# Head mixers cut into steps with preparation traced one step ahead, and TensorE held to the traced order inside them

## The chip, the cores and the metric

One core of a Trainium2 chip runs the kernel. The metric is the device time of one execution in microseconds (us); less is better. Five engines work side by side, each through its own queue of instructions: TensorE (PE, with its weight loads shown apart as PEld), VectorE (DVE), ScalarE (ACT), GpSimd (POOL) and SyncE (SP), which issues the DMAs.

## What is computed

Two layers of a sequence model over 1280 tokens (256 of context, 1024 latent) of width 1024. A layer is a mixing part and an MLP. What the change touches is the mixing part:

```python
p = modulate(x, shift, scale) @ w_in            # one projection, 20 slices
mixed = (hgrn2_mixer(p), mlstm_mixer(p), retention_mixer(p), gla_mixer(p))
# each: 4 heads, a forward and a backward chunkwise scan, summed:
#   attn = (q k^T, weighted by the decay between t and s), within a chunk
#   o    = attn @ v + (q * exp(b)) @ S          # S: state that enters the chunk
#   S    = exp(b_last) * S + (k * exp(b_last - b))^T v
x = x + g1 * (head_norm(mixed) * gates(p)) @ w_o
x = x + g2 * relu(modulate(x) @ w1)**2 @ w2
```

HGRN2 and GLA have a decay per channel, so their `attn` is built from blocks of halving size (64, 32, 16, 8, 4, 2, then pairs and the diagonal), each with its own scaled copies of q and k. Retention and mLSTM have a decay per head.

## The kernel before

All is in float32. The projections run as three matmuls a product (`mm3`, lines L294 to L296; the weights are split into a high and a low part by `whalf`: one ACT copy L282, one DVE subtraction L283). They go through `denseT` (128 output channels by 256 or 512 tokens, 24 matmuls a block, result into one of three PSUM banks, then an `evac` by ACT and DVE) and `denseV` (L632 to L634).

The mixers and the projections are interleaved by hand. A mixer is a generator that yields a cost in ns. `Fill.along` adds the cost to a debt and takes steps of queued projections (the filler) until the debt is paid; a step is what a projection does up to its own `yield`. `Fill.until` runs filler alone up to a mark. `Fill.also` is a second generator, drawn on in three of five filler steps: `ada_rows`, 128 products on DVE (L414, each with a read of its accumulator) whose 256 KB operands come by DMA, in layer 0 only, from the first HGRN2 pass on.

The passes of a layer, in the order traced, with what the filler holds: GLA (projections of HGRN2's first pair of heads and its values), HGRN2 pair 0 (`spill_hg(1)`: two decay projections and a query, then two gates), HGRN2 pair 1 (the two gates, mLSTM's keys and queries, its values, a gate), then filler alone up to mLSTM's values, two mLSTM passes, two retention passes, and the rest of the filler alone.

In `mix_vec` (GLA and HGRN2) a pass first makes the states (keys: DVE, ACT exp, transposes L893, `state_update` L818, evacuation `evac_states` L1197, a recurrence over chunks `chain` L799 and L803). Then come groups of four chunks (three for GLA). A group makes, for h = 64, 32, 16, 8, 4, 2, the scaled copies F and E (DVE L976 to L991, ACT exp L985 and L989), the products (L1000 for h = 64, L1019 below) and their place in `CTs` (DVE L1032); then `direct(1)` and `direct(0)` (L932 to L956); then the outputs: `out_chunks` multiplies the states (L831, K = 128 rows for a pair of heads, the state kept as a 128-column block whose other head's half is zero) and the values (L834, two tiles of 64 columns), and `finish` norms the result (square, matmul with `bones` L706, ACT, DVE L709) and stores it.

A scheduler of the language takes the traced instructions and fixes each engine's order ahead of the run: it plays the program through by its own costs and gives an engine the earliest traced instruction that is ready by then. So the order on TensorE is not the traced one: filler that was traced later can stand ahead of a mixer's product.

Buffers of the mixers come from `Heap`, a free list with a moving start over two long tiles (px, ph); filler weights lie in `pw`.

Of the kernel before, what the change touches and what calls it, by code (L numbers as in the profile page):

```python
# [8 lines left out]
I32 = mybir.dt.int32  # L9
# [6 lines left out]
NK = 8  # L16
# [140 lines left out]
class Fill:  # L157
# [10 lines left out]
    def step(self):  # L168
        while self.q:
# [28 lines left out]
class K:  # L198
# [36 lines left out]
    def setup(self):  # L235
# [33 lines left out]
        self.late = None  # L269
# [278 lines left out]
    SIZES = {"raw": NC * 48, "V": NC * 256, "V65": NC * 260, "S": NC * 256, "S65": NC * 130}  # L548
# [15 lines left out]
    def denseT(self, tile, tbs, evac):  # L564
# [133 lines left out]
    def finish(self, kt, ps, c0, m):  # L698
# [6 lines left out]
        p2 = self.bank(self.mb.next())[:, 0:n]  # L705
        nc.tensor.matmul(p2, lhsT=self.bones, rhs=sq, start=True, stop=True)  # L706
        nc.scalar.activation(sq, p2, AF.Ln, bias=self.eps)
        nc.scalar.activation(sq, sq, AF.Exp, scale=-0.5)
        nc.vector.scalar_tensor_tensor(y, y, self.ghead[:, self.l, kt:kt + 1], sq, op0=ALU.mult, op1=ALU.mult)  # L709
        nc.sync.dma_start(self.d_y[kt, :, 128 * c0:128 * c0 + n], y)  # L710
# [111 lines left out]
    def out_chunks(self, chunks, pair, qd, ST, at, V, kt):  # L822
# [16 lines left out]
    def mix_vec(self, S, kind):  # L839
# [29 lines left out]
        ST = self.get(S, "S")(NC, 2, 128)  # L869
        gone = [S[x] for x in (("Q", "B0", "B1") + (("G0", "G1") if hg else ("K",)))]  # L870
        gone2 = [S[x] for x in (("S",) if hg else ("S", "V"))]

        for g0, g1 in ((0, 4), (4, 8), (8, 10)):
# [3 lines left out]
            kno = [hp.alloc(n) for _ in range(2)]  # L877
            for d in range(2):
# [9 lines left out]
                if not hg:  # L888
                    nc.vector.tensor_tensor(kf, kf, Kx[:, sl], op=ALU.mult)
                bk = self.mb.next()  # L890
# [3 lines left out]
                nc.scalar.activation(self.v(kno[d], n), self.bank(bk)[:, 0:n], AF.Copy)  # L894
            bk = self.mb.next()
            for d in range(2):
                kn = self.v(kno[d], g1 - g0, 128)
                for i, c in enumerate(range(g0, g1)):
                    f = self.feeds(c, d)
                    if f is None:  # L900
                        continue
                    ps = self.state_update(c, d, kn[:, i, :], V, heads, ST, bk, d * 4 + i, 64)
            self.evac_states(bk, ST, g0, g1, 64, 4, hs)
            hp.free(*kk, *kno)
            yield (g1 - g0) * (220 + 220 * nh)
        self.chain(ST, lambda c, d: dc[d][:, c:c + 1])
# [3 lines left out]
        for g0 in range(first, NC, step):  # L910
# [4 lines left out]
            qo = [hp.alloc(n) for _ in range(2)]  # L915
            qv = [self.v(x, n) for x in qo]
            for d in range(2):
                nc.scalar.activation(qv[d], B[d][:, sl], AF.Exp, scale=esc)
                nc.vector.tensor_tensor(qv[d], qv[d], Q[:, sl], op=ALU.mult)
            ato = hp.alloc(nh * n)  # L920
            AT = self.v(ato, nh * m, 128)
            cto = hp.alloc(nh * m * 32)
            CTs = self.v(cto, nh * m, 32)

            def direct(h):
                do = hp.alloc(n)
                D = self.v(do, n)
                if h == 0 and hg:
                    ao = hp.alloc(n)
                    a = self.v(ao, n)  # L930
                    for d, o in ((0, D), (1, a)):
                        nc.vector.tensor_tensor(o, G[d][:, sl], B[d][:, sl], op=ALU.add)  # L932
                        nc.scalar.activation(o, o, AF.Exp)
# [5 lines left out]
                else:  # L939
# [12 lines left out]
                    nc.vector.tensor_tensor(D2, D2, two(Q[:, sl])[:, :, ::-1], op=ALU.mult)  # L952
# [789 lines left out]
```

## Time and profile before

| | us |
|---|---|
| median of 3 runs (lowest, highest) | 3277.83 (3273.87, 3279.31) |
| the profiled execution: its time | 3277.57 |
| its span, first to last instruction | 3275.8 |
| mixers of layer 0, about 88 to 799 us | 711 |
| mixers of layer 1, about 1873 to 2470 us | 597 |
| PE busy in the whole span | 3188.0 (97%) |
| PEld / DVE / ACT busy | 2607.3 / 2098.3 / 1285.0 |

The stages between and after the mixers (output projection, MLP) are not touched. Matmul ends are modelled, and matmuls overlap one another, so that a busy PE is not a PE at its peak. The two mixer stages are 1308 us of the span, and all that the change can move lies in them. The granted clock is 0.99 of full speed over the span.

### The profile page before, as it was taken

The numbers are of one execution on the slowest core, as the hardware profiler recorded it, in microseconds if no ns is written. First come the engines' busy times: TensorE is split into PE (matmuls) and PEld (weight loads), VectorE is DVE, ScalarE is ACT, GpSimd is POOL, SyncE is SP. The second block draws the span as 40 slices with busy tenths as digits, with TensorE's granted clock in tenths as the row PEclk, the third lists the DMA queues.
The fourth block names the chain that finished last, engine by engine and source line by source line (L and its number), as shares of the span: only waits on it lengthen the run. The fifth ranks groups of instructions, "written<-read, shape, count | busy, mean of one in ns | idle before, by whom it ended". The sixth has DMA issues, their size and how long they took to land.

```text
span 3275.8 us, 52563 instructions
## 1 busy us (share of the span) xinstructions
PE 3188.0 (97%) x20681; PEld 2607.3 (80%) x20681; DVE 2098.3 (64%) x4333; ACT 1285.0 (39%) x2665; POOL 11.5 (0%) x42
## 2 busy tenths in 40 slices
PE   7999999999999999999999999999999999999998
PEld 4787788878888888888888677788778888888887
DVE  4778887776588845454545586876756555555546
ACT  4666564545332121212122575764444322222222
POOL 0000000000000000000000000000000000000000
PEclk9999899999999999999999999999999999999999
DMA  6115566345157511111111212333224111111111
GB/s 208 58 61 176 183 186 190 120 134 179 63 165 230 161 39 39 39 39 39 39 39 40 78 64 73 120 109 113 90 72 151 58 46 52 46 52 46 52 49 65
DMA packets 181953, 308.20 MB, mean 94 GB/s; under 512 B 21880, under 2 KB 51240, under 8 KB 181448
## 3 DMA queue, kind: packets, MB, share of 16 engines
q1 hardware_dynamic: 180376, 303.02, 28.8%
q8 instruction: 162, 2.65, 0.3%
q10 hardware_dynamic: 1296, 1.81, 0.2%
q14 instruction: 87, 0.71, 0.1%
q0 software_dynamic: 32, 0.01, 0.0%
HBM read 259.11 MB, written 45.65 MB: 93 GB/s over the span
## 4 chain that ended last, share of the span: by engine, by line
PE 81%; DVE 8%; DMA 6%; ACT 3%; issue 1%; SPq 0%; DVEq 0%; ACTq 0%
PE psum L294 22%; PE psum L295 21%; PE psum L296 21%; PE psum L831 2%; PE psum L601 2%; PE psum L834 1%; PE psum L818 1%; PE psum L632 1%; DMA ph<-w_adaR 1%; PE psum L634 1%; PE psum L633 1%; PE psum L1359 1%; PE psum L706 1%; PE psum L1019 1%; DMA ps<-w_ada 1%
## 5 line engine op out<-in xcount | busy, mean ns | idle before, releaser
L526 DVE SCALAR_TENSOR_TENSOR x<-psum,st,x 128x512 f32<-128x512 f32 (+1 forms) x648 | 440.7, 689 | 203.5 <-PE psum L296 202.8
L282 ACT ACTIVATE pc<-st 128x512 fp32r<-128x512 f32 x256 | 161.2, 632 | 854.4 <-PE psum L295 840.9
L295 PE MATMUL psum<-pc,pc 128*128 128x512 f32 (+1 forms) x1296 | 477.0, 368 | 6.0 <-DVE pc L506 6.0
L294 PE MATMUL psum<-pc,pc 128*128 128x512 f32 (+1 forms) x1296 | 476.1, 367 | 0.0
L296 PE MATMUL psum<-pc,pc 128*128 128x512 f32 (+1 forms) x1296 | 474.7, 366 | 0.0
L294 PE MATMUL psum<-Hhi,pc 128*128 128x512 f32 (+1 forms) x1280 | 471.1, 368 | 1.5 <-ACT pc L282 1.5
L295 PE MATMUL psum<-Hlo,pc 128*128 128x512 f32 (+1 forms) x1280 | 472.0, 369 | 0.1
L296 PE MATMUL psum<-Hhi,pc 128*128 128x512 f32 (+1 forms) x1280 | 470.5, 368 | 0.0
L294 PE MATMUL psum<-Hhi,pw 128*128 128x512 f32 (+1 forms) x1192 | 451.5, 379 | 7.6 <-ACT pw L282 3.5
L295 PE MATMUL psum<-Hlo,pw 128*128 128x512 f32 (+1 forms) x1192 | 447.5, 375 | 0.0
L296 PE MATMUL psum<-Hhi,pw 128*128 128x512 f32 (+1 forms) x1192 | 446.6, 375 | 0.6 <-DVE pw L283 0.6
L505 DVE TENSOR_TENSOR st<-st 128x256 f32<-128x256 f32 (+1 forms) x160 | 101.8, 637 | 301.5 <-ACT pc L504 300.8
L295 PEld LDWEIGHTS psum<-pc,pc 128*128 128x128 f32 x1296 | 245.0, 189 | 48.4 <-DVE pc L506 6.9
L294 PEld LDWEIGHTS psum<-pc,pc 128*128 128x128 f32 x1296 | 245.0, 189 | 44.1 <-DVE x L526 1.2
L296 PEld LDWEIGHTS psum<-pc,pc 128*128 128x128 f32 x1296 | 244.6, 189 | 42.9 <-issue 2.7
L294 PEld LDWEIGHTS psum<-Hhi,pc 128*128 128x128 f32 x1280 | 241.3, 189 | 43.3 <-ACT pc L282 2.4
L295 PEld LDWEIGHTS psum<-Hlo,pc 128*128 128x128 f32 x1280 | 241.3, 189 | 41.0 <-issue 0.5
L283 DVE TENSOR_TENSOR pc<-st,pc 128x512 fp32r<-128x512 f32 x256 | 175.6, 689 | 153.4 <-ACT pc L282 133.5
L296 PEld LDWEIGHTS psum<-Hhi,pc 128*128 128x128 f32 x1280 | 241.1, 188 | 41.0 <-DVE pc L283 0.6
L294 PEld LDWEIGHTS psum<-Hhi,pw 128*128 128x128 f32 x1192 | 227.3, 191 | 53.7 <-issue 9.2
L296 PEld LDWEIGHTS psum<-Hhi,pw 128*128 128x128 f32 x1192 | 227.1, 191 | 39.3 <-issue 2.4
L295 PEld LDWEIGHTS psum<-Hlo,pw 128*128 128x128 f32 x1192 | 227.6, 191 | 37.7 <-issue 2.9
(401 smaller groups left out, 4859.4 us busy)
## 6 DMA issues: line engine op xcount, KB each, us to landing
st<-w_ff SPq DMA_DIRECT2D x256, 256.0 KB
ph<-w_adaR SPq DMA_DIRECT2D x128, 256.0 KB
st<-w_inT SPq DMA_DIRECT2D x96, 256.0 KB
st<-w_adaR SPq DMA_DIRECT2D x74, 256.0 KB
pc<-w_adaR SPq DMA_DIRECT2D x54, 256.0 KB
st<-w_out SPq DMA_DIRECT2D x50, 256.0 KB
d_z<-st SPq DMA_DIRECT2D x40, 256.0 KB
ps<-w_ada SPq DMA_DIRECT2D x32, 256.0 KB
```

Source lines behind the costliest of these rows:

```text
L282: nc.scalar.activation(hi, raw, AF.Copy)
L283: (eng or nc.vector).tensor_tensor(lo, raw, F(hi), op=ALU.subtract)
L294: t.matmul(out, lhsT=w[0], rhs=m[0], start=first, stop=False)
L295: t.matmul(out, lhsT=w[0], rhs=m[1], start=False, stop=False)
L296: t.matmul(out, lhsT=w[1], rhs=m[0], start=False, stop=last)
L505: nc.vector.tensor_tensor(r, r, r, op=ALU.mult)
L526: nc.vector.scalar_tensor_tensor(x, ps, self.mod[:, l, 40 + o, j:j + 1], x, op0=ALU.mult, op1=ALU.add)
L601: t.matmul(ps[:, 0:304], lhsT=h[a], rhs=u[b], start=(k + i == 0), stop=(k == NK - 1 and i == 2))
L632: t.matmul(ps[:, e, :], lhsT=h[0], rhs=u[0], start=(k == 0), stop=False)
L633: t.matmul(ps[:, e, :], lhsT=h[0], rhs=u[1], start=False, stop=False)
L634: t.matmul(ps[:, e, :], lhsT=h[1], rhs=u[0], start=False, stop=(k == NK - 1))
L831: nc.tensor.matmul(o, lhsT=ST[r0:r0 + kd, c, d, :], rhs=qd[d](c)[r0:r0 + kd, :], start=(j == 0), stop=False, tile_position=(r0, 0))
```

## The change

`mix_vec`, `mix_rt` and `mix_ml` no longer run straight on. They make a list of items (prepare, use, cost), and `staged` walks it: the next item's preparation is traced, the cost is yielded (so filler is traced), the rest of the last `finish` is traced, then the item's use. The keys, each h, the two direct parts and each `out_chunks` are items of their own; an mLSTM group is three items with 900, 900 and 400 ns a chunk in place of one with 2200, a retention group two. The sums of the costs stay, but for 600 ns at each pass's end. `finish` stops after the square and the copy, and its matmul, ACT, DVE and store come with the next item.

`denseT` yields after 12 matmuls in place of 6, and `also` is drawn on at each filler step in place of three of five. The states keep 64 columns in place of 128: `evac_states` copies once in place of twice with a mask, `chain` works on half the columns, and `out_chunks` multiplies a pair's states as two tiles, (rows of head h) by (64 columns h), in place of one. `mixers` is traced under `manual_schedule` for TensorE: inside it TensorE's instructions are issued in the order traced. The other engines stay with the scheduler.

```diff
@@ class Fill, step
             for cost in gen:
                 self.n += 1
-                if self.also and self.n % 5 in (0, 2, 4):
+                if self.also:
                     next(self.also, None)
                 return cost
@@ denseT
                     self.mm3(ps, (u[0][:, k % 4, :], u[1][:, k % 4, :]), self.hm(k, t0, n), k == 0, k == NK - 1)
-                    if k % 2 and k < NK - 1:
-                        yield 6 * n / 2.4
+                    if k == 3:
+                        yield 12 * n / 2.4
                 evac(ps, t0, n)
-                yield 6 * n / 2.4
+                yield 12 * n / 2.4
@@ finish
-        p2 = self.bank(self.mb.next())[:, 0:n]
-        nc.tensor.matmul(p2, lhsT=self.bones, rhs=sq, start=True, stop=True)
...
+        def rest():
+            p2 = self.bank(self.mb.next())[:, 0:n]
+            nc.tensor.matmul(p2, lhsT=self.bones, rhs=sq, start=True, stop=True)
...
+        self.pending = rest
+
+    def flush(self):
+        if self.pending:
+            self.pending()
+            self.pending = None
+
+    def staged(self, items):
+        st = items[0][0]()
+        for i, (_, use, cost) in enumerate(items):
+            after = items[i + 1][0]() if i + 1 < len(items) else None
+            yield cost
+            self.flush()
+            use(st)
+            st = after
+        yield 600
+        self.flush()
@@ out_chunks
             for j, d in enumerate(ds):
-                nc.tensor.matmul(o, lhsT=ST[r0:r0 + kd, c, d, :], rhs=qd[d](c)[r0:r0 + kd, :], start=(j == 0), stop=False,
-                                 tile_position=(r0, 0))
+                for h in range(2):
+                    a = r0 + kd // 2 * h
+                    nc.tensor.matmul(o[64 * h:64 * h + 64, :], lhsT=ST[a:a + kd // 2, c, d, :], rhs=qd[d](c)[a:a + kd // 2, :],
+                                     start=(j == 0), stop=False, tile_position=(a, 64 * h))
@@ mix_vec
-        ST = self.get(S, "S")(NC, 2, 128)
+        ST = self.get(S, "S")(NC, 2, 64)
...
+        for g0, g1 in ((0, 4), (4, 8), (8, 10)):
+            kno = []
+            items.append((lambda g0=g0, g1=g1: keys(g0, g1), lambda kk, g0=g0, g1=g1, kno=kno: turn(g0, g1, kk, kno),
+                          (g1 - g0) * 220))
+            items.append((lambda: None, lambda _, g0=g0, g1=g1, kno=kno: update(g0, g1, kno), (g1 - g0) * 220 * nh))
...
+            out = [(lambda h=h: prep(h), lambda st, h=h: use(h, st), m * nh * (226 if h == 64 else 124)) for h in (64, 32, 16, 8, 4, 2)]
+            out += [(lambda h=h: direct_prep(h), lambda st, h=h: direct_use(h, st), m * 220) for h in (1, 0)]
+            out += [(lambda: None, lambda _, pi=pi: outputs(pi), m * 872) for pi in range(nh // 2)]
+            return out
@@ mix_ml, the items of a group (mix_rt: queries with within, m * 550; outputs, m * 1200)
-            yield m * 2200
+            return [(weights, within, m * 900), (none, values, m * 900), (none, outputs, m * 400)]
@@ evac_states
-                if sel is None:
-                    nc.scalar.activation(ST[:, f:f + m, d, :], src, AF.Copy)
-                else:
-                    for e in range(2):
-                        nc.scalar.activation(ST[:, f:f + m, d, 64 * e:64 * e + 64], src, AF.Copy, scale=sel[:, e:e + 1])
+                nc.scalar.activation(ST[:, f:f + m, d, :], src, AF.Copy)
@@ build
-        b.mixers(l, ada)
+        with tc.manual_schedule(engines={mybir.EngineType.PE}):
+            b.mixers(l, ada)
```

## Rows read from the trace of the kernel before

**Rows 1.** The page, part 1: busy us (share of the span) and instructions.
```profile
PE 3188.0 (97%) x20681; PEld 2607.3 (80%) x20681; DVE 2098.3 (64%) x4333; ACT 1285.0 (39%) x2665; POOL 11.5 (0%) x42
```
**Rows 2.** TensorE's waits: who waited for whom, us in total, times, longest.
```profile
PE psum L1019 <- DVE px L991: 6.3, 12, 1.4
...
PE psum L818 <- ACT px L894: 2.6, 2, 2.2
```
**Rows 3.** Stretches: length, busy us of PE, PEld, DVE, ACT, POOL, granted clock, DMA.
```profile
88.00:799.00 711.00, 682.78 (x6134) 548.34 (x6133) 560.85 (x1439) 401.74 (x939) 1.53 (x14) 0.98 0.44 139
281.60:426.60 145.00, 133.65 (x1194) 106.09 (x1192) 123.01 (x312) 86.92 (x196) 0.84 (x8) 0.93 0.57 181
426.60:563.00 136.40, 131.05 (x1335) 110.83 (x1335) 111.55 (x297) 78.55 (x180) 0.45 (x4) 1.00 0.58 182
1873.00:2470.00 597.00, 583.75 (x5173) 466.15 (x5172) 427.55 (x963) 353.03 (x789) 1.60 (x14) 0.99 0.30 97
2061.00:2161.00 100.00, 99.11 (x959) 79.48 (x959) 74.42 (x152) 66.58 (x141) 0.84 (x8) 1.00 0.36 117
2161.00:2250.00 89.00, 88.30 (x929) 74.03 (x929) 63.36 (x133) 56.83 (x121) 0.45 (x4) 1.00 0.32 102
2600.00:2700.00 100.00, 100.00 (x443) 82.81 (x442) 50.61 (x73) 22.01 (x36) 0.00 (x0) 1.00 0.15 48
```
**Rows 4.** The same four HGRN2 stretches, only instructions on filler weights (tile pw).
```profile
281.60:426.60 145.00, 100.63 (x488) 76.94 (x488) 8.79 (x13) 7.52 (x12) 0.93 0.57 181
426.60:563.00 136.40, 101.48 (x603) 83.22 (x604) 9.62 (x14) 8.80 (x14) 1.00 0.58 182
2061.00:2161.00 100.00, 74.79 (x364) 56.25 (x363) 7.44 (x11) 6.31 (x10) 1.00 0.36 117
2161.00:2250.00 89.00, 68.88 (x375) 54.58 (x375) 6.81 (x10) 6.18 (x10) 1.00 0.32 102
```
**Rows 5.** The same view of line L414 alone (`ada_rows` on DVE), layer 0.
```profile
281.60:426.60 145.00, 28.98 (x84) 0.93 0.57 181
426.60:563.00 136.40, 33.76 (x98) 1.00 0.58 182
```
**Rows 6.** The same view of line L732 alone (the scan in a decay's evacuation), layer 1.
```profile
1905.00:2061.00 156.00, 11.27 (x11) 1.00 0.25 81
2061.00:2161.00 100.00, 1.22 (x1) 1.00 0.36 117
```
**Rows 7.** TensorE in order of time inside HGRN2: start, us, what ran.
```profile
360.19 0.39 PE L294 MATMUL psum<-Hhi,pw 128*128 128x512 f32 x1
360.51 0.65 PE L1019 MATMUL psum<-px 128*32 128x64 f32 x32
361.10 0.50 PE L295 MATMUL psum<-Hlo,pw 128*128 128x512 f32 x1
361.43 0.40 PE L296 MATMUL psum<-Hhi,pw 128*128 128x512 f32 x1
```
**Rows 8.** Groups by line over the span: busy us, mean ns, idle before.
```profile
L283 DVE TENSOR_TENSOR pw<-st,pw 128x512 fp32r<-128x512 f32 x154 | 104.8, 686 | 45.3 <-ACT pw L282 43.7
...
L725 DVE SCALAR_TENSOR_TENSOR st<-st,psum 128x512 f32<-128x512 f32 (+1 forms) x12 | 7.8, 653 | 0.1
```
**Rows 9.** TensorE in order of time, in the second mLSTM pass of layer 1.
```profile
2330.72 0.55 PE L1378 MATMUL psum<-st,px 128*128 128x128 f32 x3 [2.03 <-DVE px L1376]
```
**Rows 10.** TensorE in order of time, two blocks of eight `direct` products in one group.
```profile
334.09 1.05 PE L956 MATMUL psum<-st,px 128*128 128x2 f32 x8 [1.21 <-DVE px L952]
...
339.00 1.87 PE L956 MATMUL psum<-st,px 128*128 128x2 f32 x8 [3.86 <-DVE px L935]
```
**Rows 11.** TensorE in order of time: state and value products of a chunk; h = 64.
```profile
219.96 0.71 PE L831 MATMUL psum<-ph,px 64*128 64x128 f32 x4
220.60 0.44 PE L834 MATMUL psum<-px,ph 128*64 128x128 f32 x4
...
2125.52 0.69 PE L1000 MATMUL psum<-ph,px 64*64 64x64 f32 x32
```

More of the change, by code (lines that the diff above doesn't have):

```diff
@@ L898, in mix_vec, with group @@
                 for i, c in enumerate(range(g0, g1)):
[L899 to L906, printed above, removed]
+                    if self.feeds(c, d) is not None:
+                        self.state_update(c, d, kn[:, i, :], V, heads, ST, bk, d * 4 + i, 64)
+            self.evac_states(bk, ST, g0, g1, 64, 4)
+            hp.free(*kno)
+            if g1 == NC:
+                self.chain(ST, lambda c, d: dc[d][:, c:c + 1])
+        for g0, g1 in ((0, 4), (4, 8), (8, 10)):
[3 more added lines that the diff above has]
+            items.append((lambda: None, lambda _, g0=g0, g1=g1, kno=kno: update(g0, g1, kno), (g1 - g0) * 220 * nh))
         first = 0 if self.l == 0 else 2
         step = 4 if hg else 3
-        for g0 in range(first, NC, step):
+        def group(g0):
             g1 = min(NC, g0 + step)
@@ L914, in mix_vec, with direct_prep @@
             sl = slice(128 * g0, 128 * g1)
[L915 to L925, printed above, removed]
+            o = {}
+            def direct_prep(h):
                 do = hp.alloc(n)
@@ new lines, in group @@
+            out = [(lambda h=h: prep(h), lambda st, h=h: use(h, st), m * nh * (226 if h == 64 else 124)) for h in (64, 32, 16, 8, 4, 2)]
+            out += [(lambda h=h: direct_prep(h), lambda st, h=h: direct_use(h, st), m * 220) for h in (1, 0)]
+            out += [(lambda: None, lambda _, pi=pi: outputs(pi), m * 872) for pi in range(nh // 2)]
+            return out
+        for g0 in range(first, NC, step):
+            items += group(g0)
+        yield from self.staged(items)
+        hp.free(sm, *gone, *(x for x, _ in gone2))
@@ new lines, in outputs @@
+            def outputs(_):
+                AT = self.v(o["at"], 2 * m, 128)
+                qv = [self.v(x, n) for x in o["q"]]
+                qd = [lambda c, d=d: qv[d][:, 128 * (c - g0):128 * (c - g0) + 128] for d in range(2)]
+                self.out_chunks(list(range(g0, g1)), (0, 128, 2 * p), qd, ST, lambda vh, c: AT[:, (vh % 2) * m + c - g0, :], V, 4 + p)
+                hp.free(*o["q"], o["at"])
+                k = n + 128 * (first if g0 == first else 0)
+                hp.free_head(k, S["Q"], S["K"])
+                hp.free_head(k, S["S"])
@@ L1175, in mix_rt, with evac_states @@
+            return [(queries, within, m * 550), (none, outputs, m * 1200)]
+        for g0 in range(first, NC, 4):
+            items += group(g0)
+        yield from self.staged(items)
         hp.free(S["S"], S["Q"], S["K"])
-    def evac_states(self, bk, ST, g0, g1, w, per, sel=None):
+    def evac_states(self, bk, ST, g0, g1, w, per):
         nc = self.nc
@@ L1292, in mix_ml, with turn @@
         nc.gpsimd.memset(ST[:, 1, 1, :], 0.0)
-        for g0, g1 in ((0, 3), (3, 6), (6, 9), (9, 10)):
+        items = []
+        none = lambda: None
+        def turn(g0, g1, out):
             m = g1 - g0
@@ L1376, in mix_ml @@
-            nc.vector.tensor_tensor(ho[0](n), ho[0](n), ho[1](n), op=ALU.add)
-            for i in range(m):
-                nc.tensor.transpose(self.bank(bt)[:, 128 * i:128 * i + 128], HN[:, i, :], self.ident)
-            self.finish(2 + p, self.bank(bt)[:, 0:n], g0, m)
-            hp.free(w, do, *ho)
-            n += 128 * (first if g0 == first else 0)
-            hp.free_head(n, S["Q"], S["K"])
-            hp.free_head(n // 128 * 130, S["S65"])
-            yield m * 2200
+            o = {}
@@ new lines, in outputs @@
+            def outputs(_):
+                HN = self.v(o["h"][0], m, 128)
+                bt = self.obank.next()
+                for i in range(m):
+                    nc.tensor.transpose(self.bank(bt)[:, 128 * i:128 * i + 128], HN[:, i, :], self.ident)
+                self.finish(2 + p, self.bank(bt)[:, 0:n], g0, m)
+                hp.free(*o["h"])
+                k = n + 128 * (first if g0 == first else 0)
+                hp.free_head(k, S["Q"], S["K"])
+                hp.free_head(k // 128 * 130, S["S65"])
@@ L1385, in mix_ml @@
+            return [(weights, within, m * 900), (none, values, m * 900), (none, outputs, m * 400)]
+        for g0 in range(first, NC, 3):
+            items += group(g0)
+        yield from self.staged(items)
         hp.free(S["S65"], S["Q"], S["K"])
```

342 lines of the change are left out of this document (194 added, 148 removed).

## The prediction

> **What bounds the kernel now.** The page first: TensorE is busy for 97% of the span [rows 1], and the list of its waits holds only short ones, as 6.3 us in twelve before the products below h = 64 [rows 2]. The stretches come next [rows 3]. In the two mixer stages TensorE stands idle for 711.0 - 682.8 = 28 us and 597.0 - 583.8 = 13 us, so waits that the trace shows are worth 41 us at most. The rest of what can be won is in how full the busy time is. TensorE in order of time shows it [rows 7]: a filler matmul of 512 columns starts 0.226 us after the one before in a stretch of the MLP (443 in 100 us [rows 3]), but 0.32 us pass from the last filler matmul to a block of 32 mixer products, and 0.33 us from the first filler matmul after it to the second. A change from filler to mixer and back thus costs about 0.09 + 0.10 = 0.2 us. Counted in that view over both stages (the four rows of the group are one such change), there are 229 blocks of filler in layer 0 and 192 in layer 1, 421 changes, 84 us.
>
> Then the question is what else TensorE does while a mixer is not ready. The four HGRN2 stretches, cut where VectorE starts the keys of a pass, answer it [rows 3, 4]. The code allots a pass 37.2 us of filler in layer 0 and 31.2 us in layer 1 (sum of the yields). In the new steps that is 18, 18, 15 and 14 steps of 12 matmuls: 216, 216, 180 and 168 matmuls. The trace of before has 488, 603, 364 and 375 there [rows 4]. So more than half of the filler that ran beside HGRN2 was traced for later and drawn forward, because a mixer's products were not ready. VectorE is 85%, 82%, 74% and 71% busy in these stretches [rows 3]. TensorE in traced order can't draw anything forward.
>
> All sums are against the profiled execution: 3277.57 us, a span of 3275.8, 0.3 us below the median of the runs.
>
> **HGRN2 in traced order: +55.** TensorE's part of a pass: its allotted filler, 12 matmuls of 512 columns a step at 0.226 (a step of the 256-column block at an estimated 0.12 each), comes to 41.2, 41.2, 35.6 and 35.4 us. Its own products are what PE is busy beyond the filler [rows 3, 4]: 33.0, 29.6, 24.3 and 19.4. With 16, 16, 13 and 13 changes at 0.2 the pass takes 77, 74, 62 and 57 us of TensorE.
>
> VectorE's part is what it did in the stretch, less what was drawn forward. In layer 0 a product of `ada_rows` is 28.98 / 42 = 0.69 us (each counts twice [rows 5]), and 42 and 49 ran where the new steps draw 18: 16.6 and 21.4 us off. Halves of filler weights are 13, 14, 11 and 10 where 6, 6, 6 and 6 are due [rows 4], at 0.686 [rows 8]: 4.8, 5.5, 3.4 and 2.7 off. In layer 1, eleven of the twelve decay scans ran before the first stretch and one in it [rows 6], so five more belong to it: 1.02 for the scan and some four operations like the 0.65 of L725 [rows 6, 8], 18 us, of which I add half, since gates' evacuations were there in their place. That leaves 102, 85, 80 and 61 us of VectorE against 77, 74, 62 and 57: 25 + 11 + 18 + 4 = 58 us in which TensorE has nothing that it may issue. Gaps on VectorE add to that (it never was over 85% busy here), a head start in the stage before takes somewhat more from it; 55. Bounds: 20 if VectorE is ahead by a third of a group all along, since the outputs of a group give TensorE work and VectorE hardly any; 120 if VectorE again gets only 85% busy (328 / 0.85 - 270 = 116).
>
> **Chains inside an item: +52.** An mLSTM group's outputs wait for a row of small operations behind the last value product. The nearest row is a wait of 2.03 us where no filler was at hand [rows 9]. 1200 ns are yielded before the outputs, less than half a step of 2560, so in most groups no filler stands there. 14 groups (two passes of four in layer 0, of three in layer 1) at 2 us: 28; bounds 0 and 49 (3.5 each, if all operations after the last product are seen). Between the turned keys and the state products lies an evacuation; the nearest row is 2.6 us for two waits [rows 2]. 23 such places a layer, a quarter of them bare at 1.3: 14; bounds 0 and 55. The last retention pass has 12.8 us of filler in layer 0 and 10.2 in layer 1 against 27.1 and 23.6 asked for; behind that no later filler may come in. Some five items a layer at 1 us: 10; bounds 0 and 24.
>
> **What is won: -73.** The new trace has at most as many blocks of filler as yields that call for a step: walking the costs, 108 and 93 over the passes, and some four where `until` runs. 421 - 205 = 216 changes less at 0.2: -43 (25 to 60, as the change costs 0.12 or 0.28). Of the 41 us of idle time, that before mixer products falls to the new order; half, -20 (0 to 41). The state products: before, two directions take 220.60 - 219.96 = 0.64 us, and two tiles of values 0.44 at most [rows 11]. After, a direction is two tiles of half the rows and half the columns. If they go like the values, two directions take 0.88, +0.24. If they go like h = 64, whose 16 products run in four rounds of four tiles in 0.62 us or little more [rows 11], a product of 64 columns takes 0.155 and one of 128 up to 0.31, as its weights are loaded once an estimated 0.26: 0.52 to 0.62 for two directions, -0.12 to -0.02. The new tiles differ in rows as well as columns, as those of h = 64 do; I take -0.1 on 108 chunks: -10 (-13 to +26). Half the copies in `evac_states` are on ScalarE, 67% busy or less in HGRN2 [rows 3], and cost or give nothing; if it were the bound, 80 copies of some 0.4 would count, 32. Half the columns in `chain`, and the moved part of `finish`, lie on VectorE beside the rest: within the +55. `ada_rows` moves later, into the 148 filler steps left from its start; its 132 draws fit, so nothing is left for the end.
>
> The Trainium skill (TensorE: Matmul & The Clock Gate, Part 3) says that a weight load overlaps running matmuls only where the row group differs. The values' two tiles share their rows, the new ones don't, so by that rule the upper end, +26, is out and the lower one, -13, would hold: a sum of 3309 in place of 3312.
>
> Sum: +55 + 52 - 73 = +34, 3277.6 + 34 = 3312.
>
> **The rivals.**
> *Faster, 3241 (0.37).* VectorE gets ahead. Nothing holds its preparations back but buffers, and the halved states free 1280 words a partition. TensorE's long items are the outputs, beside which VectorE prepares the next group. If a third of the stalls is left, (55 + 52) / 3 = 36, the sum is 36 - 73 = -37, 3241. It decides where the stalls together fall under 73 us. For it: HGRN2's stretches of layer 1 ask only 4 and 18 us more of VectorE than of TensorE. Against it: more than half of the filler beside HGRN2 was drawn forward [rows 4].
> The Trainium skill (Perfetto Trace Analysis, Identifying the Most-Contended Engine) judges TensorE by the busy share of its weight loads and not by that of matmuls. Here that share is 83% in the MLP stretch and 77% and 78% in the mixers [rows 3], and by that rule up to 711 (1 - 0.77 / 0.83) + 597 (1 - 0.78 / 0.83) = 87 us are to be had, 3190, if nothing stalls.
> *Even slower, 3360 (0.12).* The idle gaps cost clock. After a wait of 3.86 us eight products took 1.87 us, against 1.05 before [rows 10], which is the lower of the two levels, 1.2 in place of 2.4 GHz, and the stretch has a granted clock of 0.93, the other three 1.00 [rows 3]. If these stretches, some 370 us by then, fall from 0.98 to 0.85, another 48 us go: 3360. Against it: in a stretch that waits for VectorE a slow TensorE is partly hidden.
> *No change, 3278 (0.13).* The traced order is what the scheduler had chosen, or stalls and gains cancel. The first is against the same rows [rows 4]; the second is a narrow band, 6.6 us to either side, about what a measurement of this kernel can tell from no change (0.2%).
> *The forecast, 3312 (0.38).*
>
> **How the numbers follow.** Slower by over 0.2%: 0.38 + 0.12 = 0.50. Within: 0.13. Faster: 0.37. The range takes in most of the faster rival and of the even slower one: 3215 to 3378; the forecast's own range is 3287 to 3346.
>
> **What would show it.** Right: blocks of filler in the order of time fall to about 205, with 12 or 24 matmuls each; the four HGRN2 stretches hold near 216, 216, 180 and 168 filler matmuls; TensorE's idle time there rises to some 60 us, ended by DVE (L991, L977, L932); waits of about 2 us before L1378; VectorE over 85% busy in HGRN2, and less in the stretch of filler alone behind it. Wrong: idle time of TensorE in both stages that stays under 80 us, with VectorE's preparations standing well ahead of their use; or a change between filler and mixer that costs much more or less than 0.2 us.

## The result and the profile after

The changed kernel takes 3464.37 us (median of 4 runs, 3457.69 to 3465.16) against 3276.62 us of the kernel before on the same chip: a ratio of 1.057, 95% interval 1.056 to 1.058, 188 us slower. The sign was the forecast's; the size, +34, was not, and 3464 lies outside the range of 3215 to 3378.

The page's first part after, to be set against [rows 1]:

```profile
PE 3204.1 (93%) x21089; PEld 2631.2 (76%) x21089; DVE 2090.5 (60%) x4333; ACT 1258.5 (36%) x2585; POOL 11.6 (0%) x42
```

The span is 3455.9 us. TensorE is idle for 3455.9 - 3204.1 = 251.8 us, where before it was 3275.8 - 3188.0 = 87.8: +164.0. Its busy time grew by 16.1. These two are the whole difference of the spans. The granted clock fell from 0.990 to 0.965 over the span.

TensorE's waits after, against [rows 2]: who waited for whom, us in total, times, longest.

```profile
PE psum L1084 <- DVE px L1041: 42.4, 21, 4.8
PE psum L1491 <- DVE px L1484: 30.9, 12, 4.2
PE psum L708 <- ACT st L703: 27.4, 26, 4.4
```

The first line is the 6.3 us before the products below h = 64 of before (L1019 is L1084 now), seven times as long. L1491 turns an mLSTM group's outputs (L1378 before), L708 is the matmul of `finish` (L706).

The stretches after, with the columns of [rows 3]: both mixer stages, then GLA, the two HGRN2 passes, and all from the first mLSTM pass on, in layer 0 and in layer 1.

```profile
88.00:899.00 811.00, 691.31 (x6346) 561.48 (x6345) 560.84 (x1440) 388.98 (x899) 1.63 (x14) 0.91 0.39 124
1971.00:2651.00 680.00, 592.95 (x5376) 477.81 (x5375) 420.88 (x968) 340.73 (x753) 1.66 (x14) 0.94 0.27 86
...
127.00:292.00 165.00, 132.72 (x1842) 105.90 (x1841) 120.85 (x323) 89.91 (x208) 0.00 (x0) 0.86 0.33 108
292.00:404.00 112.00, 90.04 (x956) 71.13 (x955) 92.39 (x232) 64.95 (x146) 0.00 (x0) 0.85 0.33 108
404.00:510.00 106.00, 86.47 (x967) 68.47 (x966) 89.33 (x229) 71.20 (x163) 0.52 (x4) 0.90 0.40 127
...
553.90:899.00 345.10, 301.90 (x2097) 247.24 (x2095) 210.00 (x531) 130.64 (x314) 0.27 (x2) 0.94 0.42 131
2005.00:2145.00 140.00, 117.60 (x1603) 95.08 (x1604) 100.80 (x244) 87.33 (x195) 0.00 (x0) 0.93 0.22 71
2145.00:2240.00 95.00, 74.57 (x795) 57.95 (x794) 75.60 (x165) 64.01 (x134) 0.00 (x0) 0.89 0.28 91
2240.00:2310.00 70.00, 59.44 (x712) 46.77 (x710) 58.12 (x129) 46.25 (x96) 0.21 (x2) 0.93 0.27 87
...
2367.50:2651.00 283.50, 253.43 (x1744) 205.54 (x1743) 148.62 (x342) 105.04 (x245) 0.30 (x2) 0.95 0.27 86
```

Length less PE busy is TensorE's idle time. In the stages it is 119.7 + 87.1 = 207 us, against 28 + 13 = 41 before [rows 3]. GLA holds 32.3 + 22.4 = 55 of it, the stretches from TensorE's first mLSTM operation on (553.9 and 2367.5 us) 43.2 + 30.1 = 73, and HGRN2 with the filler alone behind it 78 of the remaining 79. VectorE is 82%, 84%, 80% and 83% busy in the four HGRN2 stretches, not over 85%, so neither engine is full.

Filler in these stretches (tile pw alone), HGRN2 as in [rows 4] and then GLA:

```profile
292.00:404.00 112.00, 57.56 (x226) 44.65 (x225) 4.13 (x6) 3.77 (x6) 0.85 0.33 108
404.00:510.00 106.00, 54.22 (x237) 43.01 (x236) 4.11 (x6) 3.79 (x6) 0.90 0.40 127
2145.00:2240.00 95.00, 48.09 (x187) 36.02 (x186) 4.29 (x7) 3.92 (x7) 0.89 0.28 91
2240.00:2310.00 70.00, 39.06 (x154) 28.72 (x152) 3.24 (x5) 3.12 (x5) 0.93 0.27 87
...
127.00:292.00 165.00, 83.09 (x438) 68.80 (x437) 6.78 (x10) 6.29 (x10) 0.86 0.33 108
2005.00:2145.00 140.00, 79.54 (x432) 65.71 (x433) 7.46 (x11) 6.73 (x11) 0.93 0.22 71
```

HGRN2 holds 226, 237, 187 and 154 filler matmuls where 216, 216, 180 and 168 were forecast. GLA is what the prediction did not look at. These are the same two views of the kernel before in GLA's stretches, filler first, then all instructions:

```profile
126.00:281.60 155.60, 108.55 (x579) 84.66 (x579) 8.58 (x13) 7.86 (x13) 1.00 0.29 93
1905.00:2061.00 156.00, 114.95 (x607) 90.69 (x606) 9.50 (x14) 9.33 (x15) 1.00 0.25 81
```
```profile
126.00:281.60 155.60, 150.58 (x1903) 121.37 (x1901) 121.54 (x306) 96.43 (x220) 0.00 (x0) 1.00 0.29 93
1905.00:2061.00 156.00, 148.92 (x1695) 120.37 (x1694) 118.03 (x271) 105.71 (x231) 0.00 (x0) 1.00 0.25 81
```

Before, 579 and 607 filler matmuls stood in GLA; 438 and 432 are left, about what was traced there. With the rest gone, idle time went from 5.0 + 7.1 us to 55.

One HGRN2 group shows how a wait comes about: TensorE in order of time (start, us, what ran, wait before it), then VectorE, then three stretches with the columns of [rows 3].

```profile
315.57 0.65 PE L1084 MATMUL psum<-px 128*32 128x64 f32 x32 [1.34 <-ACT px L1065]
...
321.27 0.65 PE L1084 MATMUL psum<-px 128*32 128x64 f32 x32 [1.52 <-DVE px L1041]
325.06 1.08 PE L1084 MATMUL psum<-px 128*32 128x64 f32 x32 [3.13 <-DVE px L1041]
...
326.67 0.42 PE L296 MATMUL psum<-Hhi,pw 128*128 128x256 f32 x1
326.88 0.41 PE L294 MATMUL psum<-Hhi,pw 128*128 128x256 f32 x1
...
331.16 0.28 PE L294 MATMUL psum<-Hhi,pw 128*128 128x256 f32 x1
331.28 0.28 PE L295 MATMUL psum<-Hlo,pw 128*128 128x256 f32 x1
```
```profile
321.81 0.42 DVE L1026 TENSOR_TENSOR px<-ph 128x256 f32<-128x256 f32 x1
322.30 0.69 DVE L311 SCALAR_TENSOR_TENSOR st<-psum,st 128x512 f32<-128x512 f32 x1
322.91 0.74 DVE L1041 SCALAR_TENSOR_TENSOR px<-px,st 128x512 f32<-128x512 f32 x1
323.57 0.68 DVE L743 TENSOR_TENSOR st<-st,psum 128x512 f32<-128x512 f32 x1
324.17 0.75 DVE L1041 SCALAR_TENSOR_TENSOR px<-px,st 128x512 f32<-128x512 f32 x1
```
```profile
322.00:326.00 4.00, 0.94 (x32) 0.87 (x32) 3.92 (x7) 0.79 (x2) 0.00 (x0) 0.54 0.42 114
...
312.10:322.30 10.20, 6.97 (x147) 5.10 (x145) 8.83 (x27) 7.67 (x16) 0.00 (x0) 1.00 0.40 123
322.30:329.10 6.80, 3.94 (x44) 3.51 (x44) 6.80 (x13) 1.75 (x3) 0.00 (x0) 0.50 0.40 138
```

The products at 325.06 need both L1041. VectorE evacuates filler ahead of the first of them (L311) and between the two (L743), 1.4 us together, and TensorE, which has later filler in its program, stands idle for 3.13 us. From 322 to 326 us the granted clock is 0.54, most of it the lower of the two levels, 1.2 in place of 2.4 GHz, and filler matmuls behind it start 0.21 us apart where at 331 us it is 0.12. The lower level holds from 322.3 to 329.1 us: it begins 0.4 us into the wait of 3.13 us, so that wait as a whole can't have brought it about.

### The profile page after: what moved, and what is told of

It is laid out like the page before. It is cut to its first block, busy times and chain, and to the rows that moved or that the text cites. A ratio compares the mean times of both kernels' runs of the same rounds, so it can differ in the third digit from the quotient of the medians.

```text
span 3455.9 us, 53281 instructions
## 1 busy us (share of the span) xinstructions
PE 3204.1 (93%) x21089; PEld 2631.2 (76%) x21089; DVE 2090.5 (60%) x4333; ACT 1258.5 (36%) x2585; POOL 11.6 (0%) x42
## 4 chain that ended last, share of the span: by engine, by line
PE 76%; DVE 10%; DMA 8%; ACT 4%; issue 2%; SPq 0%; DVEq 0%; ACTq 0%; POOL 0%; POOLq 0%
PE psum L294 21%; PE psum L295 21%; PE psum L296 21%; DMA ph<-w_adaR 3%; PE psum L601 2%; PE psum L853 1%; DMA px<-d_u 1%; DVE px L1041 1%; PE psum L632 1%; PE psum L856 1%; DVE ph L414 1%; PE psum L634 1%; PE psum L633 1%; PE psum L838 1%; DMA ps<-w_ada 1%
## 5 line engine op out<-in xcount | busy, mean ns | idle before, releaser
L294 PE MATMUL psum<-Hhi,pw 128*128 128x512 f32 (+1 forms) x1192 | 478.8, 402 | 3.9 <-ACT pw L282 3.9
L296 PE MATMUL psum<-Hhi,pw 128*128 128x512 f32 (+1 forms) x1192 | 454.6, 381 | 5.0 <-DVE pw L283 5.0
L295 PE MATMUL psum<-Hlo,pw 128*128 128x512 f32 (+1 forms) x1192 | 455.5, 382 | 0.0
L294 PEld LDWEIGHTS psum<-Hhi,pw 128*128 128x128 f32 x1192 | 242.6, 204 | 55.7 <-issue 10.4
L296 PEld LDWEIGHTS psum<-Hhi,pw 128*128 128x128 f32 x1192 | 240.6, 202 | 46.9 <-DVE pw L283 5.6
L294 PEld LDWEIGHTS psum<-Hhi,pc 128*128 128x128 f32 x1280 | 241.3, 189 | 43.2 <-ACT pc L282 2.4
L295 PEld LDWEIGHTS psum<-Hlo,pw 128*128 128x128 f32 x1192 | 242.3, 203 | 35.6 <-issue 1.0
```

The lines of the kernel that those rows point to most:

```text
L294: t.matmul(out, lhsT=w[0], rhs=m[0], start=first, stop=False)
L295: t.matmul(out, lhsT=w[0], rhs=m[1], start=False, stop=False)
L296: t.matmul(out, lhsT=w[1], rhs=m[0], start=False, stop=last)
```

## The experiments

Idle time below is the span less PE busy of each run's page. Ratios are to the kernel before, run on the same chip.

| run | median us | ratio, 95% interval | idle us | PE busy us | clock |
|---|---|---|---|---|---|
| free_order | 3280.22 | 1.0016 (1.0004 to 1.0028) | 99.8 | 3176.2 | 0.988 |
| ordered_from_hgrn2 | 3413.27 | 1.043 (1.041 to 1.045) | 217.2 | 3189.7 | 0.973 |
| ordered_from_mlstm | 3358.72 | 1.026 (1.024 to 1.028) | 164.9 | 3189.3 | 0.979 |
| before_ordered | 3864.43 | 1.180 (1.177 to 1.182) | 490.7 | 3377.3 | 0.903 |
| more_filler | 3376.32 | 1.031 (1.030 to 1.033) | 199.8 | 3174.4 | 0.973 |
| mlstm_costs | 3449.22 | 1.053 (1.052 to 1.055) | 242.3 | 3204.0 | 0.966 |
| fine_steps | 3456.64 | 1.055 (1.054 to 1.057) | 233.2 | 3219.5 | 0.965 |
| two_ahead | 3430.20 | 1.048 (1.046 to 1.050) | 228.0 | 3195.9 | 0.970 |
| gla_filler | 3439.65 | 1.050 (1.047 to 1.052) | 235.5 | 3199.6 | 0.967 |
| late_rest | 3484.37 | 1.063 (1.061 to 1.066) | 276.9 | 3202.4 | 0.962 |
| rest_at_once | 3464.71 | 1.057 (1.055 to 1.059) | 256.2 | 3207.1 | 0.963 |
| all_cures | 3380.50 | 1.031 (1.029 to 1.034) | 202.9 | 3181.8 | 0.970 |
| all_cures_free | 3254.75 | 0.993 (0.990 to 0.995) | 99.8 | 3159.9 | 0.987 |
| cures_ordered | 3356.41 | 1.024 (1.022 to 1.026) | 175.0 | 3175.8 | 0.973 |
| cures_free | 3249.63 | 0.991 (0.989 to 0.993) | 88.5 | 3162.8 | 0.988 |
| ada_later | 3467.91 | 1.058 (1.055 to 1.062) | 255.5 | 3210.1 | 0.963 |
| ada_narrow | 3465.72 | 1.056 (1.054 to 1.058) | 252.5 | 3211.2 | 0.962 |
| vector_ordered | 3785.01 | 1.154 (1.151 to 1.156) | 494.0 | 3299.3 | 0.925 |

**Is it the order, and where?** Four kernels: the change without the order, with the order from a later pass on, and the order alone.

```diff
 free_order (before_ordered is the reverse edit on the kernel before)
-        with tc.manual_schedule(engines={mybir.EngineType.PE}):
-            b.mixers(l, ada)
+        b.mixers(l, ada)
 ordered_from_hgrn2: inside mixers, from this line to the end
+        with self.tc.manual_schedule(engines={mybir.EngineType.PE}):
             self.feat_hg(hg[0])
 ordered_from_mlstm: the same from
             V = self.get(ml[0], "V65")(NC, 260)
```

> The changed kernel with TensorE given back to the scheduler in the mixers; all else of the change stays. Theory O (the traced order is the loss: TensorE may not draw later filler forward while a product waits): TensorE's idle time in the two mixer stages falls from some 207 us to 40 or less, the clock there returns to 0.98, and the time to that of the kernel before or a little below, 3240 to 3290 us. Rival S (the split itself costs: coarser filler steps, more items, rests of finish that come late): the time stays above 3400 us. Between 3300 and 3400 both carry a part.

> The changed kernel, the traced order only from the first HGRN2 pass of a layer to the end of its mixers; GLA is free. Theory O with the stalls read by stage (GLA 44 and 40 us above TensorE's own work, which the prediction had at nothing): 3464 less some 84, 3370 to 3400 us. Rival H (the loss belongs to HGRN2, whose passes ask most of VectorE, as the prediction had it, and GLA's gaps only shift it): 3440 us or more.

> The changed kernel, the traced order only from the first mLSTM pass of a layer on; GLA and HGRN2 are free. Theory O by stage: mLSTM and retention cost some 25 to 50 us beside a free order, so 3270 to 3320 us, and the step to the run with the order from HGRN2 on is some 80 to 110 us. Rival M (the chains inside the mLSTM groups are the larger part, as large as HGRN2): 3350 us or more.

> The kernel before with the traced order on TensorE in the mixers and nothing else of the change. Theory O: no preparation stands ahead there, so each product meets its whole chain of DVE and ACT; at least as slow as the changed kernel, 3464 to 3700 us. The distance to the changed kernel is what the split and the preparation ahead give under the order. Rival S (the split costs, the order does not): near the kernel before, 3260 to 3310 us.

Without the order the change takes 3280 us, within 0.2% of the kernel before, so the order is the loss and the split is not. What the split wins there in busy time, 3188.0 - 3176.2 = 12 us, it loses in idle time (99.8 - 87.8), and it does so in HGRN2, where TensorE is idle for 31 us against 18 before. Read by stage, the order costs 78 us from mLSTM on (3358.72 - 3280.22), 55 more with HGRN2, and 51 more with GLA (46 by the ratios). Rival H falls, as GLA's part is its own, though 3413 is also above the 3400 that theory O gave at most. Rival M stands: I expected at most 3320 with the order from mLSTM on, and that part is the largest. The order alone on the kernel before costs 589 us and gives 3864, above the 3700 expected at most. So under the order all the rest of the change together is worth 400; no run takes the split, the preparation ahead and the halved states apart.

**More filler beside the waits.**

```diff
 more_filler
-RATIO = (1.0, 1.0, 1.0, 1.0, 1.0)
+RATIO = (1.0, 1.7, 1.7, 1.8, 1.0)
 gla_filler: RATIO = (1.35, 1.0, 1.0, 1.0, 1.0), and
+        m1 = fill.add(*self.spill_hg(1))
         fill.along(self.mix_vec(gl, "gl"), RATIO[0])
-        m1 = fill.add(*self.spill_hg(1))
```

> The changed kernel, but an HGRN2 pass asks 1.7 times and an mLSTM pass 1.8 times the filler for its costs (GLA and retention as they are), so that the some 245 us of filler that ran alone behind these passes stand among their products instead. Theory F (the waits lie where too little filler was traced; the chains of DVE and ACT go on meanwhile): idle time of TensorE in HGRN2 and mLSTM falls by half, and the time to 3390 to 3420 us. Rival V (VectorE sets these passes, and the added filler brings it its own halves and evacuations): 3450 to 3480 us.

> The changed kernel, but GLA asks 1.35 times the filler (the stretch of before held 579 filler matmuls in layer 0 where the changed kernel holds 438), with the second pair's projections of HGRN2 queued ahead of GLA in place of behind it. Theory F (GLA waits because the filler that was drawn into it before is gone): GLA's 55 us of idle time in both layers fall by half, 3430 to 3445 us. Rival Q (the filler is only taken from what stands beside HGRN2 or alone, where the same time is lost again; or DVE's queue makes the waits): 3455 us or more.

Beside HGRN2 and mLSTM it gave 88 us, more than expected, beside GLA 25, as expected, though GLA's idle time fell by a quarter only (55 to 41 us) and not by half. Idle time fell by 52 us with more_filler, and PE's busy time fell by 30 as well, as the clock rose from 0.965 to 0.973. HGRN2 with the filler alone behind it, from TensorE's first operation of the pass to that of mLSTM, in layer 0 and layer 1, first in the changed kernel, then in more_filler:

```profile
293.90:553.90 260.00, 215.94 (x2207) 176.30 (x2206) 195.62 (x501) 144.43 (x325) 1.35 (x12) 0.90 0.42 134
2146.50:2367.50 221.00, 186.80 (x1867) 150.89 (x1866) 141.80 (x306) 127.25 (x268) 1.35 (x12) 0.93 0.31 99
...
292.80:530.50 237.70, 214.94 (x2255) 174.18 (x2254) 198.14 (x503) 146.80 (x330) 1.36 (x12) 0.95 0.46 151
2109.20:2300.50 191.30, 176.91 (x1867) 142.81 (x1866) 143.28 (x306) 126.02 (x268) 1.35 (x12) 0.98 0.35 115
```

The work is nearly the same, only the filler that ran alone behind the passes now stands among their products. TensorE is idle there for 23 + 14 = 37 us in place of 44 + 34 = 78, so here it is less than half; from mLSTM on it fell only from 73 to 64. VectorE does the same work in 238 and 191 us that took 260 and 221. So VectorE's amount of work didn't set these passes.

**mLSTM's bare outputs.**

```diff
 mlstm_costs
-            return [(weights, within, m * 900), (none, values, m * 900), (none, outputs, m * 400)]
+            return [(weights, within, m * 700), (none, values, m * 500), (none, outputs, m * 1000)]
```

> The changed kernel with the costs of an mLSTM group's three items at 700, 500 and 1000 ns a chunk in place of 900, 900 and 400: the sum is nearly the same, but 3000 ns stand before a group's outputs, more than a filler step of 2560. If the 30.9 us that TensorE waits before the turned outputs (twelve waits on the last DVE operation) come from the missing filler there, they fall under 10 us and the time by 15 to 30 us, to 3434 to 3450. If the waits only move to the value products or to the next group, the time stays within 6 us of 3464.

The time is 15 us less, and the wait fell from 30.9 us:

```profile
PE psum L1491 <- DVE px L1484: 9.2, 6, 2.6
```

Of 22 us won there 15 show in the time and 9.5 in the idle time of the profiled execution, as other waits of mLSTM's grew.

**Lead.** `staged` holds two prepared items in place of one, where the buffers allow.

```diff
 two_ahead, in staged (hold: the first items of groups; near: 1 in GLA, 6 in HGRN2)
-            after = items[i + 1][0]() if i + 1 < len(items) else None
+            while len(st) < min(i + 3, len(items)) and (len(st) == i + 1 or (len(st) not in hold and ...
+                st.append(items[len(st)][0]())
...
```

> The changed kernel with preparations traced two items ahead in place of one, where the buffers hold it: all of GLA's groups but the first item of each, and the direct parts of HGRN2. Theory A (one item of preparation is too short a lead): the waits of GLA, 54 us of idle time in both layers, fall by a third or more, 3440 or less. Rival V (the order and the load of VectorE decide, whichever item the preparation is traced in, since VectorE's own order is the scheduler's): within 8 us of 3464.

34 us less, 24 of them idle time: GLA's fell from 55 to 38 us, HGRN2's from 78 to 67, and from mLSTM on it rose by 6. A longer lead pays, though VectorE's own order is the scheduler's.

**The price of a change between filler and mixer.**

```diff
 fine_steps, in denseT (and also in three of five again)
-                    if k == 3:
-                        yield 12 * n / 2.4
+                    if k % 2 and k < NK - 1:
+                        yield 6 * n / 2.4
                 evac(ps, t0, n)
-                yield 12 * n / 2.4
+                yield 6 * n / 2.4
```

> The changed kernel with the filler steps of before (6 matmuls a step, ada_rows drawn in three of five), the traced order kept. More items get filler in front, and there are more changes between filler and mixer: walking the costs, some 100 blocks more, 200 changes. If a change costs 0.2 us and waits stay as they are: +40, 3500. If the even spread covers the waits better than that: under 3464, down to 3430.

Counted in the order of time, blocks of filler rose from 108 + 96 to 148 + 126, by 70 and not by 100. PE's busy time rose by 15.4 us, 0.22 a block, which agrees with the 0.2 taken from [rows 7]. But TensorE also worked 204 us at the lower clock in place of 190; if that cost half of the 14, a block is 0.12. Idle time fell by 18.6. The two nearly cancel: 8 us less in the time, 3 in the span.

**`finish`.** Once with its rest traced behind the next item's products, once undeferred.

```diff
 late_rest, in staged (finish itself flushes an older rest first)
-            self.flush()
+            old = self.pending
             use(st)
+            if self.pending is old:
+                self.flush()
 rest_at_once, at the end of finish
-        self.pending = rest
+        rest()
```

> The changed kernel with the rest of finish traced behind the next item's products in place of ahead of them, so that its matmul has those products, too, between itself and the square on ScalarE. TensorE waits 27 us in 26 places there. If they go: 3440 to 3450 us. If the wait only shows at another instruction, since ScalarE is late for the next products as well: within 8 us of 3464.

> The changed kernel with finish run at once, as before the change: its matmul right behind the square on ScalarE, under the traced order. 54 calls of finish (27 a layer at most) at some 1.5 to 2 us of bare wait for the square, less the 27 us that TensorE waits there now: +30 to +70 us, 3495 to 3535, if the deferral covers. If the deferral covers nothing: within 8 us of 3464.

The first missed both of its bands: the late rest cost 20 us. Its waits (L709 there is the matmul of `finish`):

```profile
PE psum L709 <- ACT st L704: 27.4, 17, 4.7
PE psum L709 <- ACT px L1068: 16.9, 6, 4.4
...
PE psum L709 <- DVE px L1462: 13.2, 4, 4.5
```

The wait for the square is as long as it was, and new ones follow, for the ACT copy of the h = 64 products and for DVE reads of mLSTM's. The matmul takes its PSUM bank from the same four banks (4 to 7) as these products and so meets a bank that is still read. Undeferred, the time is the same to 0.3 us, which is the second band, that the deferral covers nothing:

```profile
PE psum L708 <- ACT st L703: 34.8, 48, 3.7
```

48 waits of 0.7 us in place of 26 of 1.05: the deferral saves half of the waits and 7 us of waiting, nothing in the time.

**All cures, with and without the order.** all_cures takes more filler (1.35, 1.5, 1.5, 1.8), two_ahead, mlstm_costs and late_rest together; cures_ordered leaves late_rest out and has 1.7 for HGRN2; the two _free runs are the same kernels without `manual_schedule`.

> The traced order kept, with all at once: more filler beside GLA (1.35), HGRN2 (1.5) and mLSTM (1.8), the second pair's projections queued early, two items of preparation ahead in GLA, mLSTM's costs at 700, 500 and 1000, the rest of finish late. If the gains add up (88, 34, 15, and some 25 for GLA and finish, less a third that they share): 3464 less 100 to 150, 3310 to 3365 us. If each wait that goes uncovers the next: 3365 or more. Below 3275, the kernel before, only if nearly all waits go, since some 206 changes there and back at 0.2 us are what the traced order saves.

> The same kernel with TensorE given back to the scheduler in the mixers. Theory O: the scheduler covers waits by drawing forward whatever is traced, so where the filler is traced hardly matters to it: 3260 to 3290 us, as the changed kernel in free order, 3280. If the distribution of filler was the loss and not the order, it would gain here too, by 50 us or more.

> The traced order with the cures that gained: filler 1.35 beside GLA, 1.7 beside HGRN2, 1.8 beside mLSTM, the second pair's projections queued early, two items of preparation ahead in GLA, mLSTM's costs at 700, 500 and 1000; the rest of finish as in the changed kernel. If the gains add up: 3464 - 88 - 34 - 15 - 24 = 3303; with a third shared 3355. If it comes near 3280, the loss was where filler and preparation were traced; if it stays above 3330, the larger part belongs to the order as such, which no such spread repairs.

> The same in the scheduler's order. Under free order the late rest should cost little, since the scheduler can put filler in front of it: 3250 to 3265, as the run with all cures in free order (3255).

all_cures came out in its second band, 3365 or more. cures_ordered, without the late rest and with 1.7 in place of 1.5 for HGRN2, is 24 us faster; the runs don't tell which of the two did it. In cures_ordered the gains share: 108 us together (3464.37 - 3356.41), of 162 that the single runs add up to. What is left waits at the same places:

```profile
PE psum L708 <- ACT st L703: 25.9, 21, 6.3
PE psum L1084 <- DVE px L1041: 19.5, 11, 6.1
...
PE psum L1492 <- DVE px L1485: 10.6, 4, 5.7
```

The order costs 107 us (3356.41 - 3249.63) even where filler and lead are traced for it. So the larger part of the loss that was left belongs to the order as such. The same kernel in free order has the lowest time of the study, 0.991 of the kernel before (0.989 to 0.993), from which all_cures_free (0.990 to 0.995) can't be told. Both are a little faster than expected: in free order, too, the spread and the lead give 25 to 31 us against free_order, though not 50.

**VectorE's amount of work or its order?** Layer 0's `ada_rows` was moved behind HGRN2, then narrowed to an eighth of its columns (the other seven eighths of its sums are left out), and VectorE put in traced order.

```diff
 ada_later: fill.also = ada(...) stands ahead of the mLSTM passes
 ada_narrow
-nc.vector.scalar_tensor_tensor(w, w, 1.0, c, op0=...
+nc.vector.scalar_tensor_tensor(w[:, 0:64], w[:, 0:64], 1.0, c[:, 0:64], op0=...
 vector_ordered
-manual_schedule(engines={mybir.EngineType.PE})
+manual_schedule(engines={mybir.EngineType.PE, mybir.EngineType.DVE})
```

> The changed kernel, but ada_rows is drawn on from the first mLSTM pass on in place of the first HGRN2 pass, so that its products of 0.69 us leave VectorE's queue in GLA and HGRN2 of layer 0 (21 ran in GLA's stretch, 31 in HGRN2's: 36 us). If VectorE's amount of work paces TensorE there: 20 us or more off, 3444 or less, the rest at the stage's end. If the latency of the chains does it: within 8 us of 3464.

> The changed kernel, but each product of ada_rows works on 64 of its 512 columns (seven eighths of these sums are left out): the number of instructions and the DMAs stay, their 69 us on VectorE in layer 0's mixers (14, 21 and 33 us in GLA, HGRN2 and behind) fall to some 20. If VectorE's amount of work paces TensorE: the 35 us of GLA and HGRN2 in good part, 3440 or less. If the chains' latency and order do it: 3456 or more.

> The changed kernel with VectorE, too, in traced order inside the mixers. Theory Q (TensorE waits because the scheduler put a filler's evacuation or a product of ada_rows in front of the preparation that TensorE needs next): the preparation then stands in front of the filler's, the idle time falls by a quarter or more, 3420 or less. Rival W (VectorE in traced order waits for TensorE's filler and for DMAs with preparations queued behind): 3500 or more. In between, place in the queue matters little.

ada_later decides nothing, as 42 and 54 instructions of L414 still ran in GLA and HGRN2 (42 and 62 in the changed kernel). ada_narrow does. L414 on VectorE in the changed kernel, then there:

```profile
127.00:292.00 165.00, 14.42 (x42) 0.86 0.33 108
292.00:510.00 218.00, 21.30 (x62) 0.88 0.37 117
```
```profile
127.00:292.00 165.00, 4.88 (x46) 0.86 0.33 105
292.00:510.00 218.00, 7.90 (x71) 0.86 0.40 126
```

23 us of VectorE went from these stretches and the time stayed (3465.72): that work filled gaps in its queue. vector_ordered was far slower, since preparations then stand behind evacuations that wait; VectorE waits 152.9 us, with its own part of a filler's evacuation, for ScalarE's (18.6 in the changed kernel), and TensorE's wait for L1041 grows from 42.4 to 154.7 us:

```profile
DVE st L311 <- ACT st L309: 152.9, 45, 8.3
```
```profile
PE psum L1084 <- DVE px L1041: 154.7, 44, 9.3
```

So VectorE's order matters much, and the load that `ada_rows` adds doesn't. This run does not settle theory Q: an order that puts preparations ahead of filler's evacuations without making VectorE wait was not tried, and in the group shown such evacuations stand between the preparations.

## Why the prediction was right in sign and wrong in size

The sign had a chance of 0.50 on record, so that it came out right says little.

**What held.** Nothing may be drawn forward: the filler in HGRN2 fell to what is traced there. Blocks of filler are 204, forecast 205, so the -43 is borne out as a count; its price is 0.2 us a change by [rows 7] and 0.12 to 0.22 by fine_steps. In the state products, eight of 64 columns take 0.58 us where four of 128 took 0.64 [rows 11]:

```profile
347.07 0.65 PE L853 MATMUL psum<-px,ph 64*64 64x128 f32 x8
347.65 0.44 PE L856 MATMUL psum<-px,ph 128*64 128x128 f32 x4
```

That is 0.06 less on each of 108 chunks, -6, where I took -10.

The Trainium skill (TensorE: Matmul & The Clock Gate, Part 3) has a weight load overlap running matmuls only where the row group differs, and by it the term was to be -13; the sign is the rule's, the size half of it. The other page that the prediction named (Perfetto Trace Analysis, Identifying the Most-Contended Engine) would, as the prediction read it, have had weight loads, at 77% and 78% of the mixer stages, leave up to 87 us to be had; under the order they fell to 561.48 / 811 = 69% and 477.81 / 680 = 70%.

**The step that failed: stalls were priced only where I had cut stretches.** The argument from drawn-forward filler was made for HGRN2 and not for GLA, which carried no term. GLA's own rows show the same surplus, 579 and 607 against 438 and 432. It was worth 55 - 12 = 43 us of idle time, and 51 us of time in ordered_from_hgrn2 against the full order.

**HGRN2, +55, came near in size by luck, and its mechanism was wrong.** Idle time in HGRN2 and the filler alone behind it is 78 us, where before the four stretches held 18 [rows 3]: +60, of which 13 are there without the order, too (31 in free_order). But VectorE's total against TensorE's total isn't why. VectorE is 80 to 84% busy; less work on it gave nothing (ada_narrow), the same filler moved among the products halved the idle time (more_filler), and preparations traced earlier took 11 us of it (two_ahead). What the rows show is uneven pace within a group: over the halvings VectorE is nearly full (3.92 of 4 us in the window shown) and TensorE has 0.94 us of work, since an item asks only 124 ns a chunk and head, 992, of filler. That each chain's latency sets the wait fits all of these; it is argued from the order of time, not measured alone, and no run separates it from filler's evacuations that stand in the chain on VectorE.

**Chains, +52, were nearly right as idle time and short as time.** From mLSTM on, TensorE is idle for 73 us, before some 41 - 18 - 12 = 11: +62. The mLSTM outputs take 30.9 us in twelve waits, 28 in fourteen forecast. In the time the order costs 78 there, 65 of idle and 13 of busy time (ordered_from_mlstm against free_order). A slip that moves nothing: a quarter of 46 places at 1.3 us is 15 and not 14, and all of them 60 and not 55.

**-20 for waits of before was no gain.** I let half of the old idle time vanish. It grew everywhere.

**The clock was a rival and should have been a term.** In filler matmuls of 512 columns, counted in the order of time, two that start 0.36 to 0.50 us apart are 15 before and 185 after, at 0.426 in place of 0.229: 170 x 0.197 = 33 us, on top of the stalls. That leaves out all other work at the lower level. The trace has the lower level for 242 us of the span, 66 before, with TensorE busy for 190 of them, 50 before. Were all that work half as long at the upper level, the clock would cost 95 - 25 = 70 us, an upper estimate. The rival gave 48 for it, at 0.12, and only for HGRN2.

Together: predicted idle time 41 - 20 + 55 + 52 = 128, measured 207, 79 short (some 43 in GLA, 20 in the waits of before, 10 in the chains, 5 in HGRN2); states 4. Of the 146 us between 3312 and the profiled execution's time, 3457.69, 63 are left, in PE's busy time. They lie between the two figures for the clock, 33 and 70, so the clock may be all of them; how they divide between it and the price of a change isn't shown. The range failed by its form: with the gains as forecast the upper bounds of the stalls, 120 + 49 + 55 + 24 = 248, give 3278 + 248 - 73 = 3453, and I took the even slower rival, 3360, for its end.

## What to carry to other kernels

A fixed order on one engine has to be paid wherever the scheduler drew work forward: count filler executed against filler traced in every stage, not only in the one that looks worst, and price each bare chain and the lower clock behind it. Under such an order, where filler is traced decides (88 us here), so it should be allotted by what the slowest engine needs for an item and not by the item's TensorE time; more_filler only scaled the allotment, so that this is advice and not a result. Under the scheduler's order the same spread and lead still gave 0.9% over the kernel before, by runs that don't tell which of them did it.

## What the runs showed of the hardware

In the group shown the granted clock stood at the upper level from 312.1 to 322.3 us, while TensorE was busy for 6.97 of 10.2 us and waited for 1.34 and 1.52 us. It then stood at the lower one to 329.1 us, with TensorE busy for 3.94 of 6.8 us, and the filler in that stretch ran at about half pace (0.21 us from start to start in place of 0.12).

Over a whole run the clock falls as idle time grows, but not by its sum alone: 0.988 at 100 us, 0.970 to 0.973 at 175 to 228, 0.965 at 252, and 0.903 and 0.925 at 491 and 494 (before_ordered, vector_ordered).
